# Rotary products on VectorE, row scaling and weight loads on ScalarE, and a reordered start, in an attention and retention block

## The chip, the cores and the metric

The kernel runs on one core of a Trainium2 chip. The metric is the device time of one execution in microseconds; for the kernel before, the median of three runs is 2031.37 us (2030.02, 2031.37 and 2033.79).

## What is computed

One encoder layer on 2048 tokens of width 1024, in fp32: a normalised input, one wide projection, a chunked attention branch, a retention branch whose queries and keys are rotated, and a gated merge.

```python
h = rms_norm(x, norm_gain)
q_a, k_a, v_a, g_a, q_r, k_r, v_r, g_r, m_a, m_r = split_columns(h @ w_in)
o_a = chunk_band_attention(q_a, k_a, v_a, rel_bias)
branch_a = (o_a * silu(g_a)) @ w_out_attn
qr, kr = rotary(q_r, positions), rotary(k_r, positions)
# rotary: concatenate [x1 * cos - x2 * sin, x1 * sin + x2 * cos]
o_r = retention_chunkwise(qr, kr, v_r, gn_gain)
branch_r = (o_r * silu(g_r)) @ w_out_ret
x = x + (sigmoid(m_a) * branch_a + sigmoid(m_r) * branch_r) @ w_out
return rms_norm(x, final_gain)
```

## The kernel before

**Split arithmetic.** Each fp32 operand of a large matmul is kept as a high half (a cast, `wh`) and a low half (the difference, `wl`), and three matmuls of halves replace one. `make` does this for a weight: the cast on ScalarE, the difference on VectorE or GpSimd `LO_LAG` = 4 steps later.

**Projection.** `w_in` is multiplied in chunks of 256 columns for 1024 tokens by Strassen's scheme: seven products of 12 matmuls a chunk (`PRODUCTS`). The activation parts stand ready in `R[0..6]`; the weight parts are two blocks of the raw weights or sums of them (`SUMS_OF`, t1 to t4, on GpSimd). Raw weights come by `load`, two loads a chunk of 512 KB into a ring of `RAWS` = 3 buffers, 9 and 8 products ahead (`RAW_LEADS`). The jobs are p0 and g0 for the first 1024 tokens, p1 and g1 for the second, and resident jobs for the output weights.

**Order of the work.** All engines' instructions are issued in program order through wrappers (`Ordered`, line 137 in the profile). One generator runs the products; `step()` issues three matmuls, a quarter of a product, and then whatever is due. `later(n, fn)` defers work by n steps, `put(lag, dst, src)` issues a store on SP that many steps later, `run_to(n)` runs steps up to n, and `prime(n)` prepares the weights of the first n products (in the running stretch three ahead, `AHEAD`).

**Start.** `start_up` takes the first 1024 tokens as xa and xb (512 each). Per block of 512 it squares the rows, forms the inverse root on VectorE (`chain`), scales the rows, transposes them on TensorE and writes the parts: `hi` and `lo` make R[0] to R[2], s1 to s3 the sums, and `to_parts` their halves. The second activation part's low half is called r11 below (`r_84` in the order's rows); s2 becomes s4 by subtracting the two halves of R[1] on GpSimd, eight operations.

**Second half.** During p0, `second_half` squares the other 1024 tokens and, in four pieces, fetches their rows (`xs`, 128x512), scales them on GpSimd, transposes them ten steps later (`pst`), combines and stores them; `reload` reads them back before p1.

**Rotation.** `ep_rotated` is run when both halves of a group of query or key columns are out of PSUM. For block b (512 tokens): two cross products with the sine table on GpSimd (t, 3 steps later), two own products with the cosine table (steps 7 and 8) and two sums (9 and 10) on VectorE. `keys` then transposes the rotated keys on TensorE in two halves (`trkr`, steps 15 and 19), and `parted` splits and stores them. The two blocks of a chunk pair follow each other, the odd one first. There are 16 rotations, eight of them of keys.

Of the kernel before, what the change touches and what calls it, by code (L numbers as in the profile page):

```python
# [21 lines left out]
P = 128  # L22
# [34 lines left out]
ATT_FILLS = (1.0, 1.0)  # L57
PV_LAG = 3
RET_FILLS = (2.1, 2.3)
RAW_LEADS = (9, 8)  # L60
TR_LATER = 16
YR_FROM = 14
# [5 lines left out]
def hybrid_kernel(  # L68
# [186 lines left out]
    class Chunk:  # L255
# [7 lines left out]
        def load(self, js=None):  # L263
            self.raw = self.raw or []
            for j in range(self.job.kh) if js is None else js:
                raw = wp.tile([P, 4, T], F32, tag="raw", bufs=RAWS, name=f"raw_{self.job.name}_{self.c}_{j}")
                dma(raw, self.job.stream(self.c, j))
                self.raw.append(raw)

        def half(self, j, c):  # L270
# [217 lines left out]
    def start_up():  # L488
# [88 lines left out]
        a11 = [E(f"a11_{k}") for k in range(4)]  # L577
        for k in range(4):
            act.activation(a11[k], ps[k], AF.Copy, scale=ng[:, k:k + 1])
        squares(xb, "b", 1, True)  # L580
        run_to(4)
        squares(xb, "b", 2, True)
        prime(3)
        ps = [TR(f"pa1_{k}") for k in range(4)]
        for k in range(4):
            turn(ps[k], k, xa, 1)
            hi(1, k, ps[k], 4 + k)
            lo(1, k, ps[k], 4 + k)
        for i in range(2):
            ch[1].b[f"b2{i + 1}"] = E(f"b2{i + 1}", shape=(P, 4, P))  # L590
        quarter(1, "b21")
# [4 lines left out]
        run_to(8)  # L596
        prime(4)
        a21 = [E(f"a21_{k}") for k in range(4)]
        squares(xb, "b", 3)
        run_to(12)  # L600
        tiny = ACC("tiny")
        nn["b"][1] = tiny[:, 0:4]
        chain("b", 0, 4)
        for f in (1, 0):
            for t in range(4):
                scale(xb, "b", t, f, t % 2)
        for dst in (0, 1, 3):
            ch[0].sum(*SUMS_OF[dst])
        run_to(16)
# [45 lines left out]
        for c in range(2):  # L655
            ch[c].sum(*SUMS_OF[2], E)
        run_to(28)
        for k in range(4):
            to_parts(5, k, s3[k])
        prime(9)  # L660
        for k in range(4):
            pool.tensor_tensor(s2[k], r32(R[1][0][:, k, :]), s2[k], ALU.subtract)
            pool.tensor_tensor(s2[k], r32(R[1][1][:, k, :]), s2[k], ALU.add)
        run_to(32)
        prime(10)
        for k in range(4):
            to_parts(3, k, s1[k])
        prime(11)
# [7 lines left out]
    def second_half(at):  # L676
# [25 lines left out]
        def piece(k):  # L702
            tiles = {}

            def fetch(i, f):
                a = tiles[i, f] = E(f"xs_{k}_{i}_{f}", shape=(P, 4, P))
                rows = x[0, (2 + i) * B:(3 + i) * B, 512 * f + k * P:512 * f + (k + 1) * P]
                dma(a, rows.rearrange("(t p) c -> p t c", p=P))
                later(8, lambda: scale(i, f))

            def scale(i, f):
                a = tiles[i, f]
                r = rs[:, 4 * i:4 * i + 4].unsqueeze(2).broadcast_to([P, 4, P])
                pool.tensor_tensor(a, a, r, ALU.mult)
                later(10, lambda: turn(i, f))

            def turn(i, f):
                a = tiles[i, f]
                ps = TR(f"pst_{k}_{i}_{f}")
                for t in range(4):  # L720
                    pe.transpose(ps[:, t * P:(t + 1) * P], a[:, t, :], ident)
                a = tiles[i, f] = a.rearrange("p t c -> p (t c)")
                later(1, lambda: act.activation(a, ps, AF.Copy, scale=ng[:, 4 * f + k:4 * f + k + 1]))

            def store(m, t, lag):
                put(lag, cscr[m][k], t)

            def first():
                s1 = tiles["s1"] = E(f"s1_{k}")
                pool.tensor_tensor(s1, tiles[1, 0], tiles[1, 1], ALU.add)  # L730
                store(2, tiles[1, 1], 2)
                store(3, s1, 4)

            def second():
                a11 = tiles[0, 0]
                s2 = tiles["s2"] = E(f"s2_{k}")
                dve.tensor_tensor(s2, tiles["s1"], a11, ALU.subtract)
# [12 lines left out]
            fetch(1, 0)  # L750
            later(3, lambda: fetch(1, 1))
            later(6, lambda: fetch(0, 0))
            later(10, lambda: fetch(0, 1))
            later(24, first)
            later(28, second)
            later(32, third)
# [42 lines left out]
    def ep_qa(cc, b, j, src, ps):  # L799
        p = 2 * cc + j  # L800

        def go():
            qh, ql = two(f"qa_{b}_{p}")
            act.mul(qh, src, -0.125)

            def rest():
                dve.scalar_tensor_tensor(ql, src, -0.125, r32(qh), ALU.mult, ALU.subtract)
                put(3, r32(qascr[p][b][:, :, 0, :]), halves(qh))
                put(3, r32(qascr[p][b][:, :, 1, :]), halves(ql))

            soon(2, rest)

# [2 lines left out]
    def ep_ka(cc, b, j, src, ps):  # L815
        p = 2 * cc + j

        def go():
# [3 lines left out]
            def rest():  # L822
                dve.tensor_tensor(kl, src, r32(kh), ALU.subtract)
                for i in range(2):
                    put(3, r32(kascr[2 * p + i][b][0:64, :]), r32(kh[64 * i:64 * i + 64, :]))
                    put(3, r32(kascr[2 * p + i][b][64:128, :]), r32(kl[64 * i:64 * i + 64, :]))

            soon(2, rest)

# [10 lines left out]
    def ep_va(cc, b, j, src, ps):  # L840
# [3 lines left out]
        def rest():  # L844
# [6 lines left out]

            def low(i):
                dve.tensor_tensor(vt[i][:, :, HD:P], pv[:, i], r32(vt[i][:, :, 0:HD]), ALU.subtract)
                put(3, r32(vascr[2 * p + i][b]), r32(vt[i]).rearrange("p t c -> p (t c)"))

            for i in range(2):
                later(1 + i, lambda i=i: high(i))
# [15 lines left out]
    def ep_rotated(kind):  # L873

        def epilogue(cc, b, j, src, ps):
# [7 lines left out]
            nm = f"{kind}_{cc}_{b}"  # L883
            ts = [E(f"t{n}_{nm}") for n in range(2)]

            def cross():
                for n in range(2):
                    pool.tensor_tensor(ts[n], xs[1 - n], s, ALU.mult)

            def own(n):  # L890
                dve.tensor_tensor(xs[n], xs[n], c, ALU.mult)
# [1 line left out]
            def both(n):  # L893
                dve.tensor_tensor(xs[n], xs[n], ts[n], ALU.add if n else ALU.subtract)

            later(3, cross)
            for n in range(2):
                later(7 + n, lambda n=n: own(n))
                later(9 + n, lambda n=n: both(n))
            (keys if kind == "k" else queries)(cc, b, xs, nm)  # L900

        return epilogue

    def parted(xs, nm, at, eng, dst):
# [7 lines left out]
        def low(n):  # L912
            eng.tensor_tensor(ws[n][1], xs[n], r32(ws[n][0]), ALU.subtract)
            for i in range(2):
                put(4, dst(i, n), halves(ws[n][i]))

        for n in range(2):
            later(at + n, lambda n=n: high(n))
            later(at + 4 + 2 * n, lambda n=n: low(n))

    def queries(cc, b, xs, nm):
        parted(xs, nm, 13, dve, lambda i, h: r32(qrscr[cc][b][:, :, :, h, i]).rearrange("u i c t -> (i c) u t"))

    def keys(cc, b, xs, nm):
        parted(xs, nm, 13, pool, lambda i, h: r32(krscr[cc][b][:, i, :, :, h]).rearrange("u i c t -> (i c) u t"))

        def turn(u):
            pk = TR(f"trkr_{nm}_{u}")
# [11 lines left out]
            def low(n):  # L940
                dve.tensor_tensor(
                    kt[n][:, :, :, HD:P], pk[:, 2 * n:2 * n + 2], r32(kt[n][:, :, :, 0:HD]), ALU.subtract
                )
                put(4, r32(kdscr[2 * cc + n][b][:, u]), r32(kt[n]).rearrange("p i t c -> p i (t c)"))

            for n in range(2):
                later(2 + n, lambda n=n: high(n))
                later(5 + n, lambda n=n: low(n))

        for u in range(2):  # L950
            later(15 + 4 * u, lambda u=u: turn(u))

    def ep_vr(cc, b, j, src, ps):
        h = 2 * cc + j
# [3 lines left out]
        def rest():  # L958
# [16 lines left out]
            def low():  # L975
                pool.tensor_tensor(vv[1], vc, r32(vv[0]), ALU.subtract)
                for n in range(2):
                    put(3, r32(vrscr[h][b][:, :, n, :]), r32(vv[n]))

            later(2, centred)  # L980
            later(4, high)
# [761 lines left out]
```

## Time and profile before

| | us |
|---|---|
| median of three runs | 2031.37 |
| profiled execution | 2029.79 |
| its span | 2028.0 |
| TensorE busy | 1937.3 |
| VectorE busy | 1363.4 |
| ScalarE busy | 881.5 |
| GpSimd busy | 943.1 |

The span runs from the first to the last instruction of one profiled execution; busy times are of that span. Most operations are recorded under the line of the wrapper that issues them, so rows are told apart by tile names: `wh_p` and `wl_p` are halves of weights of the p jobs, `t_p` the sums, `raw_p` the raw weights, `ps_p_x` and its kin the products' accumulators, `r` the activation parts, `u_p`, `c_p` and `xk` columns on their way out, `cs_k` the tables, `t_k` the cross products, `trkr_k` the transposed keys. The names in front of an arrow are outputs, those behind it inputs.

### The profile page before, as it was taken

What the parts mean: (1) busy time and instruction counts of PE and PEld (TensorE: products, weight loads), DVE (VectorE), ACT (ScalarE), POOL (GpSimd) and SP (SyncE); (2) the same over time, 40 slices, a digit from 0 to 9 for tenths busy, and PEclk for the clock granted to TensorE, in tenths of its full rate; (3) what the DMA queues carried; (4) which work ended last, traced back from release to release, by engine and by line L of the source; (5) the groups of instructions that cost most, each with busy time, mean ns of one, the idle gap of its engine ahead of it and who ended that gap; (6) DMA issues with size and microseconds to landing.
All of it is one profiled execution on the core that took longest, in us unless ns stands there. A gap on an engine that the chain in (4) does not pass through costs nothing.

```text
span 2028.0 us, 30428 instructions
## 1 busy us (share of the span) xinstructions
PE 1937.3 (96%) x9712; PEld 1611.1 (79%) x9712; DVE 1363.4 (67%) x2571; ACT 881.5 (43%) x1759; POOL 943.1 (47%) x765
## 2 busy tenths in 40 slices
PE   5899999999999999999999999999999999999998
PEld 4677777888888887777787888887888777888886
DVE  7968677677766667878777767765556644643554
ACT  5444343465555555333333555554455311322221
POOL 2644855555555676556664454454665134021000
PEclk9899999999999999999999999999999999999999
DMA  5376686755638887676784645554998899976664
GB/s 166 97 253 192 209 277 222 203 156 161 181 120 278 277 280 251 213 242 220 230 291 154 200 144 156 168 156 121 285 280 267 299 374 366 358 243 207 197 197 135
DMA packets 340912, 447.45 MB, mean 221 GB/s; under 512 B 30776, under 2 KB 194256, under 8 KB 340752
## 3 DMA queue, kind: packets, MB, share of 16 engines
q1 hardware_dynamic: 339712, 445.50, 68.9%
q8 instruction: 78, 1.28, 0.3%
q14 instruction: 82, 0.67, 0.1%
q10 hardware_dynamic: 1040, 0.00, 0.0%
HBM read 294.50 MB, written 150.89 MB: 220 GB/s over the span
## 4 chain that ended last, share of the span: by engine, by line
PE 77%; DVE 10%; DMA 5%; issue 4%; POOL 2%; ACT 1%; SPq 1%; DVEq 0%; POOLq 0%; ACTq 0%
PE ps_g_z L137 7%; PE ps_g_x L137 6%; PE ps_p_x L137 5%; PE ps_p_z L137 5%; PE po L137 4%; PE wide L137 3%; PE ps_g_w L137 3%; PE ps_g_v L137 3%; PE ps_g_y L137 3%; PE ps_p_w L137 3%; PE ps_p_v L137 3%; PE o L137 3%; PE tp L137 2%; PE ps_p_y L137 2%; DVE wl_p L137 2%
## 5 line engine op out<-in xcount | busy, mean ns | idle before, releaser
L137 POOL TENSOR_SCALAR pr<-pr,rsum 128x640 f32<-128x640 f32 (+4 forms) x128 | 96.5, 754 | 235.6 <-DVE rsum L137 98.6
L137 PE MATMUL ps_p_x<-r,wh_p 128*128 128x512 f32 x448 | 144.9, 404 | 4.3 <-DVE r L137 4.3
L137 PE MATMUL ps_p_z<-r,wh_p 128*128 128x512 f32 x448 | 141.7, 396 | 2.7 <-ACT wh_p L137 1.4
L137 PE MATMUL ps_g_z<-r,wh_g 128*128 128x512 f32 x448 | 142.4, 399 | 1.7 <-DVE c_g L137 1.3
L137 DVE CUSTOM_DVE_ANT_0 pr<-wide,bt 128x640 f32<-128x640 f32 (+4 forms) x128 | 94.3, 737 | 72.9 <-PE wide L137 65.2
L137 PE MATMUL ps_g_x<-r,wh_g 128*128 128x512 f32 x448 | 142.6, 399 | 0.0
L137 POOL TENSOR_TENSOR t_p<-raw_p,t_p 128x512 f32<-128x512 f32 x52 | 75.8, 1458 | 132.1 <-DVE wl_p L137 91.4
L137 ACT ACTIVATE pr<-pr,mn 128x640 f32<-128x640 f32 (+4 forms) x128 | 98.0, 766 | 80.5 <-DVE mn L137 80.5
L137 DVE TENSOR_TENSOR ptl<-tp,pth 128x384 fp32r<-128x384 f32 x168 | 95.7, 571 | 37.4 <-ACT pth L137 36.6
L137 ACT CAST pth<-tp 128x384 fp32r<-128x384 f32 x168 | 85.3, 514 | 75.5 <-PE tp L137 67.1
L137 DVE TENSOR_TENSOR wl_p<-t_p,wh_p 128x512 fp32r<-128x512 f32 x112 | 114.1, 1018 | 0.5 <-ACT wh_p L137 0.4
L1090 POOL TENSOR_TENSOR gr<-gr,ta 128x512 f32<-128x512 f32 x32 | 45.8, 1431 | 141.2 <-DVE gr L1089 81.6
L137 POOL TENSOR_TENSOR sl<-sm,sh 128x512 fp32r<-128x512 f32 x64 | 88.1, 1377 | 38.9 <-ACT sh L137 29.7
L137 PEld LDWEIGHTS ps_p_x<-r,wh_p 128*128 128x128 f32 x448 | 84.9, 193 | 22.8 <-DVE r L137 5.6
L137 PEld LDWEIGHTS tp<-ident,pr 128*128 128x128 f32 x560 | 69.6, 140 | 36.5 <-DVE ptl L137 8.5
L137 PEld LDWEIGHTS ps_p_z<-r,wh_p 128*128 128x128 f32 x448 | 82.1, 188 | 20.1 <-ACT wh_p L137 1.9
L137 PE MATMUL tp<-ident,pr 128*128 128x128 f32 x560 | 90.0, 274 | 7.4 <-DVE g L137 2.9
L137 PE MATMUL ps_p_x<-r,wl_p 128*128 128x512 f32 x224 | 89.7, 400 | 6.9 <-DVE wl_p L137 6.9
L137 PE MATMUL wide<-ka,qa 128*128 128x512 f32 (+2 forms) x448 | 94.0, 326 | 0.7 <-DVE mn L137 0.7
L137 DVE TENSOR_TENSOR sm<-sr,dm 128x512 f32<-128x512 f32 x64 | 44.2, 690 | 73.6 <-PE sr L137 43.9
L137 PE MATMUL po<-pth,va 128*128 128x256 f32 x336 | 92.7, 298 | 0.0
L137 ACT CAST wh_p<-t_p 128x512 fp32r<-128x512 f32 x112 | 69.1, 619 | 48.2 <-PE ps_p_z L137 24.0
(1183 smaller groups left out, 5930.2 us busy)
## 6 DMA issues: line engine op xcount, KB each, us to landing
raw_g<-in_w_in_dram SPq DMA_DIRECT2D x56, 512.0 KB, 5.2
raw_p<-in_w_in_dram SPq DMA_DIRECT2D x52, 512.0 KB, 5.0
qa<-qas SPq DMA_DIRECT2D x128, 128.0 KB, 2.9
qr<-qrs SPq DMA_DIRECT2D x128, 128.0 KB, 4.3
vr<-vrs SPq DMA_DIRECT2D x64, 256.0 KB, 4.4
ka<-kas SPq DMA_DIRECT2D x40, 256.0 KB, 3.4
va<-vas SPq DMA_DIRECT2D x40, 256.0 KB, 3.4
kds<-kdt_k SPq DMA_DIRECT2D x32, 256.0 KB, 5.0
```

The source lines that it names most:

```text
L137: return tc.keep_in_program_order(op(*a, **k))
L1090: pool.tensor_tensor(g, g, ta, ALU.add)
```

## The change

1. Rotary: the two cross products move to VectorE, one step apart. With `late` = 0 for odd blocks and 4 for even ones, a rotation's six operations stand at steps late + 1 to late + 6, the splitting at late + 8 (it was 13), the transposes at late + 11 and late + 14 (they were 15 and 19).
2. Rows of the second half are scaled on ScalarE, 128 columns at a time, and transposed six steps later instead of ten.
3. The raw weights of the Strassen jobs are loaded from ScalarE's queue, 108 loads; those of the resident jobs stay on SP.
4. Stores of queries, keys, values and parts are issued six steps after they are formed (three or four before), those of the second half's pieces four steps later.
5. In `start_up`, squares of two tiles of xb move behind r11, the inverse root and the row scales ahead of a run of steps, the preparation of products 9 and 10 ahead of and between the halves of part 5, and the second column block's values are kept (`a12`, four copies on ScalarE) so that s4 takes four GpSimd operations.

```diff
+ROT_LATE = 4
+PUT = 6
...
-                dma(raw, self.job.stream(self.c, j))
+                (dma if self.job.resident else act.dma_start)(raw, self.job.stream(self.c, j))
...
-        squares(xb, "b", 1, True)
         run_to(4)
-        squares(xb, "b", 2, True)
         prime(3)
...
             hi(1, k, ps[k], 4 + k)
             lo(1, k, ps[k], 4 + k)
+        a12 = [E(f"a12_{k}") for k in range(4)]
...
         a21 = [E(f"a21_{k}") for k in range(4)]
+        squares(xb, "b", 1, True)
         squares(xb, "b", 3)
-        run_to(12)
+        squares(xb, "b", 2, True)
         tiny = ACC("tiny")
         nn["b"][1] = tiny[:, 0:4]
         chain("b", 0, 4)
+        for k in range(4):
+            act.activation(a12[k], ps[k], AF.Copy, scale=ng[:, 4 + k:5 + k])
         for f in (1, 0):
             for t in range(4):
                 scale(xb, "b", t, f, t % 2)
+        run_to(12)
...
         run_to(28)
+        prime(9)
         for k in range(4):
             to_parts(5, k, s3[k])
-        prime(9)
+            if k == 1:
+                prime(10)
         for k in range(4):
-            pool.tensor_tensor(s2[k], r32(R[1][0][:, k, :]), s2[k], ALU.subtract)
-            pool.tensor_tensor(s2[k], r32(R[1][1][:, k, :]), s2[k], ALU.add)
+            pool.tensor_tensor(s2[k], a12[k], s2[k], ALU.subtract)
         run_to(32)
-        prime(10)
...
-                r = rs[:, 4 * i:4 * i + 4].unsqueeze(2).broadcast_to([P, 4, P])
-                pool.tensor_tensor(a, a, r, ALU.mult)
-                later(10, lambda: turn(i, f))
+                for t in range(4):
+                    later(t // 2, lambda t=t: act.mul(a[:, t], a[:, t], rs[:, 4 * i + t:4 * i + t + 1]))
+                later(6, lambda: turn(i, f))
...
-                put(lag, cscr[m][k], t)
+                put(lag + 4, cscr[m][k], t)
...
-                put(3, r32(qascr[p][b][:, :, 0, :]), halves(qh))
+                put(PUT, r32(qascr[p][b][:, :, 0, :]), halves(qh))
...
-            def cross():
-                for n in range(2):
-                    pool.tensor_tensor(ts[n], xs[1 - n], s, ALU.mult)
+            def cross(n):
+                dve.tensor_tensor(ts[n], xs[1 - n], s, ALU.mult)
...
-            later(3, cross)
+
+            late = 0 if b % 2 else ROT_LATE
             for n in range(2):
-                later(7 + n, lambda n=n: own(n))
-                later(9 + n, lambda n=n: both(n))
-            (keys if kind == "k" else queries)(cc, b, xs, nm)
+                later(late + 1 + n, lambda n=n: cross(n))
+                later(late + 3 + n, lambda n=n: own(n))
+                later(late + 5 + n, lambda n=n: both(n))
+            (keys if kind == "k" else queries)(cc, b, xs, nm, late)
...
-        parted(xs, nm, 13, pool, lambda i, h: r32(krscr[cc][b][:, i, :, :, h]).rearrange("u i c t -> (i c) u t"))
+    def keys(cc, b, xs, nm, late):
+        parted(xs, nm, late + 8, pool, lambda i, h: r32(krscr[cc][b][:, i, :, :, h]).rearrange("u i c t -> (i c) u t"))
...
-            later(15 + 4 * u, lambda u=u: turn(u))
+            later(late + 11 + 3 * u, lambda u=u: turn(u))
```

How the instructions stand is shown at three places. The first is VectorE at the first rotation of keys (`u_p_2_1229` and `c_p_2_1231` are the odd block's halves; `u_p_2_1152` and `xk_0_0_1250` the even block's; the wrapper's line is 137 before and 139 after). Before:

```order
L137 TENSOR_TENSOR u_p_2_1229<-ps_p_2_w,u_p_2_1229 128x512
L137 TENSOR_TENSOR wl_p_3_4_1257<-t_p_3_1190,wh_p_3_4_1256 128x512
L137 TENSOR_TENSOR u_p_2_1152<-ps_p_2_z,u_p_2_1152 128x512
L137 TENSOR_TENSOR wl_p_3_1_1287<-t_p_3_1192,wh_p_3_1_1286 128x512
L137 TENSOR_TENSOR u_p_2_1229<-u_p_2_1229,cs_k_1_0_1182 128x512
L137 TENSOR_TENSOR c_p_2_1231<-c_p_2_1231,cs_k_1_0_1182 128x512
L137 TENSOR_TENSOR u_p_2_1229<-u_p_2_1229,t_k_1_1277 128x512
L137 TENSOR_TENSOR wl_p_3_2_1310<-t_p_3_1214,wh_p_3_2_1309 128x512
L137 TENSOR_TENSOR c_p_2_1231<-c_p_2_1231,t_k_1_1278 128x512
L137 TENSOR_TENSOR xk_0_0_1250<-xk_0_0_1250,cs_k_0_0_1279 128x512
```

After:

```order
L139 TENSOR_TENSOR wl_p_3_4_1261<-t_p_3_1194,wh_p_3_4_1260 128x512
L139 TENSOR_TENSOR t_k_1_1281<-c_p_2_1235,cs_k_1_1_1183 128x512
L139 TENSOR_TENSOR t_k_1_1282<-u_p_2_1233,cs_k_1_1_1183 128x512
L139 TENSOR_TENSOR u_p_2_1233<-u_p_2_1233,cs_k_1_0_1182 128x512
L139 TENSOR_TENSOR c_p_2_1235<-c_p_2_1235,cs_k_1_0_1182 128x512
L139 TENSOR_TENSOR u_p_2_1154<-ps_p_2_z,u_p_2_1154 128x512
L139 TENSOR_TENSOR u_p_2_1233<-u_p_2_1233,t_k_1_1281 128x512
L139 TENSOR_TENSOR wl_p_3_1_1292<-t_p_3_1196,wh_p_3_1_1291 128x512
L139 TENSOR_TENSOR c_p_2_1235<-c_p_2_1235,t_k_1_1282 128x512
L139 TENSOR_TENSOR t_k_0_1312<-u_p_2_1154,cs_k_0_1_1284 128x512
L139 TENSOR_TENSOR wl_p_3_2_1317<-t_p_3_1218,wh_p_3_2_1316 128x512
L139 TENSOR_TENSOR t_k_0_1313<-xk_0_0_1254,cs_k_0_1_1284 128x512
```

The odd block's rotation is complete one weight's low half earlier, and its cross products stand on the same engine ahead of the own ones.

The second place is GpSimd there, after the change (`t_p` are sums of weights, `l_k` low halves of rotated keys):

```order
L139 TENSOR_TENSOR t_p_3_1294<-raw_p_3_1_1097,t_p_3_1196 128x512
L139 TENSOR_TENSOR l_k_1_0_1332<-u_p_2_1233,h_k_1_0_1331 128x512
L139 TENSOR_TENSOR t_p_4_1381<-raw_p_4_0_1258 128x512
L139 TENSOR_TENSOR t_p_4_1383<-raw_p_4_1_1289,t_p_4_1381 128x512
L139 TENSOR_TENSOR l_k_1_1_1340<-c_p_2_1235,h_k_1_1_1339 128x512
```

Before, four `t_k` products stood behind the first of these rows, and the first `l_k` operation behind both sums `t_p_4`.

The third is ScalarE at the same place, where the loads of the next chunk's raw weights now stand among the casts:

```order
L139 ACTIVATE xn_1_1173,ss_1011<-xn_1_1173 128x512
L139 DMA raw_p_4_0_1258<-in_w_in_dram 128x4x256
L139 CAST wh_p_3_4_1260<-t_p_3_1194 128x512
L139 DMA raw_p_4_1_1289<-in_w_in_dram 128x4x256
L139 CAST wh_p_3_1_1291<-t_p_3_1196 128x512
L139 CAST wh_p_3_2_1316<-t_p_3_1218 128x512
```

Before, both loads stood on SP between stores, tables and rows, and the casts followed one another.

## Rows read from the trace of the kernel before

**Rows 1.** The page's first lines: span, busy time by engine, the chain that ended last

```profile
span 2028.0 us, 30428 instructions
...
PE 1937.3 (96%) x9712; PEld 1611.1 (79%) x9712; DVE 1363.4 (67%) x2571; ACT 881.5 (43%) x1759; POOL 943.1 (47%) x765
...
PE 77%; DVE 10%; DMA 5%; issue 4%; POOL 2%; ACT 1%; SPq 1%; DVEq 0%; POOLq 0%; ACTq 0%
```

**Rows 2.** Windows of TensorE: start:end, length us, busy (instructions), granted clock, DMA share, GB/s

```profile
0.00:75.00 75.00, 46.85 (x177) 0.89 0.38 112
...
75.00:350.00 275.00, 258.75 (x1192) 0.98 0.71 224
...
800.00:1100.00 300.00, 281.85 (x1258) 0.98 0.72 234
```

**Rows 3.** Tile t_k (rotary products): count, ns min/median/max, starts; last, who waited (us, times)

```profile
L137 POOL TENSOR_TENSOR t_k<-u_p,cs_k x8: 1277/1733/1757, 108.0 to 1000.4; 128x512 f32<-128x512 f32 x8
...
L137 DVE TENSOR_TENSOR u_p<-u_p,t_k x8: 676/1212/1772, 112.1 to 1011.3; 128x512 f32<-128x512 f32 x8
...
  PE trkr_k L137: 14.4, 9
```

**Rows 4.** TensorE's waits: tile, releaser, us in total, times, longest us

```profile
PE ps_p_v L137 <- DVE wl_p L137: 7.1, 5, 4.1
...
PE ps_p_x L137 <- DVE wl_p L137: 6.9, 5, 2.6
...
PE ps_p_x L137 <- DVE r L137: 4.3, 1, 4.3
...
PE pst L137 <- POOL xs L137: 3.5, 2, 3.1
```

**Rows 5.** TensorE's timeline, 28 to 71: start, us, operation, [idle before it <- releaser]

```profile
30.73 0.80 PE L137 MATMUL ps_p_x<-r,wh_p 128*128 128x512 f32 x1 [4.26 <-DVE r L137]
...
31.75 1.05 PE L137 MATMUL ps_p_x<-r,wh_p 128*128 128x512 f32 x2
...
34.09 0.62 PE L137 MATMUL ps_p_x<-r,wh_p 128*128 128x512 f32 x2
...
36.84 0.61 PE L137 MATMUL ps_p_x<-r,wh_p 128*128 128x512 f32 x2
...
39.21 4.90 PE L137 MATMUL p<-ident,xb 128*128 128x128 f32 x24 [1.52 <-DVE xb L137]
...
68.75 0.79 PE L137 MATMUL ps_p_v<-r,wl_p 128*128 128x512 f32 x1 [4.05 <-DVE wl_p L137]
```

**Rows 6.** VectorE's timeline, from the start and from the first rotation of keys

```profile
26.60 1.75 DVE L137 CUSTOM_DVE_ANT_0 junk<-xb 128x512 bf16<-128x512 f32 x1
...
35.61 0.69 DVE L137 SCALAR_TENSOR_TENSOR l_qa<-ps_p_x,h_qa 128x512 fp32r<-128x512 f32 x1 [2.37 <-ACT h_qa L137]
...
62.96 4.06 DVE L137 TENSOR_TENSOR r<-s,r 128x512 fp32r<-128x512 f32 x4
...
110.43 1.79 DVE L137 TENSOR_TENSOR c_p<-c_p,cs_k 128x512 f32<-128x512 f32 x1
```

**Rows 7.** GpSimd's timeline, the same stretches

```profile
57.59 6.01 POOL L137 TENSOR_TENSOR a<-r,a 128x512 f32<-128x512 f32 x4 [0.63 <-DVE r L137]
...
108.05 3.62 POOL L137 TENSOR_TENSOR t_k<-u_p,cs_k 128x512 f32<-128x512 f32 x2
```

**Rows 8.** Tile xs (rows of the second half): the scaling

```profile
L137 POOL TENSOR_TENSOR xs<-xs,rs x16: 1032/1040/1488, 205.9 to 323.4; 128x512 f32<-128x512 f32 x16
```

**Rows 9.** ScalarE's timeline, two sizes of cast

```profile
102.87 0.61 ACT L137 CAST wh_p<-t_p 128x512 fp32r<-128x512 f32 x1
...
120.72 0.36 ACT L137 CAST kdt_k<-trkr_k 128x256 fp32r<-128x256 f32 x1
```

**Rows 10.** Tile raw_p (raw weights): the issues of its loads

```profile
L137 SPq DMA_DIRECT2D raw_p<-in_w_in_dram x52: 367/384/1547, 44.2 to 1058.6; - x52
```

**Rows 11.** SP's queue, its waits: releaser, us in total, times, longest us

```profile
SPq L137 <- DVE wl_p L137: 44.7, 28, 12.3
```

More of the change, by code (lines that the diff above doesn't have):

```diff
@@ L807, in rest @@
                 dve.scalar_tensor_tensor(ql, src, -0.125, r32(qh), ALU.mult, ALU.subtract)
-                put(3, r32(qascr[p][b][:, :, 0, :]), halves(qh))
-                put(3, r32(qascr[p][b][:, :, 1, :]), halves(ql))
+                put(PUT, r32(qascr[p][b][:, :, 0, :]), halves(qh))
+                put(PUT, r32(qascr[p][b][:, :, 1, :]), halves(ql))
             soon(2, rest)
@@ L824, in rest @@
                 for i in range(2):
-                    put(3, r32(kascr[2 * p + i][b][0:64, :]), r32(kh[64 * i:64 * i + 64, :]))
-                    put(3, r32(kascr[2 * p + i][b][64:128, :]), r32(kl[64 * i:64 * i + 64, :]))
+                    put(PUT, r32(kascr[2 * p + i][b][0:64, :]), r32(kh[64 * i:64 * i + 64, :]))
+                    put(PUT, r32(kascr[2 * p + i][b][64:128, :]), r32(kl[64 * i:64 * i + 64, :]))
             soon(2, rest)
@@ L853, in low @@
                 dve.tensor_tensor(vt[i][:, :, HD:P], pv[:, i], r32(vt[i][:, :, 0:HD]), ALU.subtract)
-                put(3, r32(vascr[2 * p + i][b]), r32(vt[i]).rearrange("p t c -> p (t c)"))
+                put(PUT, r32(vascr[2 * p + i][b]), r32(vt[i]).rearrange("p t c -> p (t c)"))
             for i in range(2):
@@ L914, in low @@
             for i in range(2):
-                put(4, dst(i, n), halves(ws[n][i]))
+                put(PUT, dst(i, n), halves(ws[n][i]))
         for n in range(2):
@@ L919, in parted, with queries @@
             later(at + 4 + 2 * n, lambda n=n: low(n))
-    def queries(cc, b, xs, nm):
-        parted(xs, nm, 13, dve, lambda i, h: r32(qrscr[cc][b][:, :, :, h, i]).rearrange("u i c t -> (i c) u t"))
-    def keys(cc, b, xs, nm):
-        parted(xs, nm, 13, pool, lambda i, h: r32(krscr[cc][b][:, i, :, :, h]).rearrange("u i c t -> (i c) u t"))
+    def queries(cc, b, xs, nm, late):
+        parted(xs, nm, late + 8, dve, lambda i, h: r32(qrscr[cc][b][:, :, :, h, i]).rearrange("u i c t -> (i c) u t"))
+    def keys(cc, b, xs, nm, late):
+        parted(xs, nm, late + 8, pool, lambda i, h: r32(krscr[cc][b][:, i, :, :, h]).rearrange("u i c t -> (i c) u t"))
         def turn(u):
@@ L943, in low @@
                 )
-                put(4, r32(kdscr[2 * cc + n][b][:, u]), r32(kt[n]).rearrange("p i t c -> p i (t c)"))
+                put(PUT, r32(kdscr[2 * cc + n][b][:, u]), r32(kt[n]).rearrange("p i t c -> p i (t c)"))
             for n in range(2):
@@ L977, in low @@
                 for n in range(2):
-                    put(3, r32(vrscr[h][b][:, :, n, :]), r32(vv[n]))
+                    put(PUT, r32(vrscr[h][b][:, :, n, :]), r32(vv[n]))
             later(2, centred)
```

## The prediction

> **What bounds the kernel now.** I read the page first: TensorE is busy 1937.3 of 2028.0 us, VectorE 1363.4, ScalarE 881.5, GpSimd 943.1, and the chain that ended last runs 77% over TensorE and 10% over VectorE [rows 1]. So no engine but TensorE is full, and a change of the other engines' work can win only what TensorE idles, about 91 us, and what it loses at its lower clock. The windows tell where that lies [rows 2]: the first 75 us (46.85 busy, clock 0.89), the first 1024 tokens' projection from 75 to 350 us (258.75 of 275, clock 0.98), and the second 1024 tokens' from 800 to 1100 us (281.85 of 300, clock 0.98). Idle there is 28.2, 16.3 and 18.2 us. The change edits these stretches and little else. Everything after them hangs on TensorE too, so what is won there should stay won.
>
> Then the waits, by what ended them. The tile view of the rotary products shows TensorE waiting 14.4 us in 9 places at the transposes of the rotated keys, the largest single item in the two projections [rows 3]. The list of TensorE's waits adds 7.1 and 6.9 us for low halves of weights, 3.5 us for scaled rows of x, and in the start 4.3 us for the low half of the second activation part [rows 4].
>
> **The start.** Removed from in front of r11 on VectorE are four squares of xb, each about 1.75 us (the last of them in [rows 6]), 6.8 us in a row; they now stand behind it. TensorE's 4.26 us wait at 30.73 ended by r11 [rows 5], so it goes. The squares are then in front of the norm of xb instead, but so they were before, and the norm also stood behind a low half that waited 2.37 us for ScalarE and began at 35.61 [rows 6]; it now stands ahead of it. With VectorE free 6.8 us earlier, the squares, the norm and the row scales end some 3 to 4 us earlier, and the transposes of xb, which began at 39.21 [rows 5], follow. I take 3.6 us, between 1.4 and the 4.26 of the wait. Four new ScalarE copies (a12) cost 4 x 0.6 us there, beside the norm on VectorE; if that cover is gone, they delay half of the row scales by at most 2.4 us, which is the lower end.
>
> Later in the start, the low half of a weight lands 4.05 us late at 68.75 [rows 5], behind four low halves of an activation part that took VectorE 4.06 us [rows 6]. Moving the preparation of products 9 and 10 among these takes two to four of the four away from in front: 3 us, with 0 and 4 as ends. Forming s2 in four GpSimd operations instead of eight saves one of two stretches of about 6 us [rows 7]; a wait follows only partly from it, and I take 0.9 (0 to 2). Together the start gives 7.5 us, between 4 and 12.
>
> **The rotations.** Removed are 32 GpSimd products, of 1.28 to 1.76 us [rows 3], and 32 come to VectorE. On VectorE an operation with both inputs in SBUF takes 0.68 us at its fastest and 1.77 us at its slowest in the same eight instructions [rows 3]: it is slow where a GpSimd product runs beside it, as the one at 110.43, 1.79 us, beside two that run from 108.05 to 111.67 [rows 6, 7]. That is 1.1 us per overlap. Before, a pair of key rotations is 8 VectorE operations, about half of them slow: 4 x 1.77 + 4 x 0.68 = 9.8 us, and each pair also waits for GpSimd's products to end. Now it is 12 operations: 8.2 us if all are fast. So VectorE does more instructions in less time. Odd blocks have their six operations at steps 1 to 6 and the transposes at 11; a step is three matmuls, a quarter of a product of 2.75 us (from 34.09 to 36.84 [rows 5]), so they have some 2.7 us of slack. Even blocks have steps 5 to 10 and 15. But the order puts sums of the next weights and the low half of the odd block's keys on GpSimd in that stretch; three such overlaps cost 3.3 us, and the even blocks should still be 1 to 3 us late. Of the 14.4 us I leave 4.5: 10 us won, between 0 and 14.4.
>
> On this the Trainium skill, "SBUF — State Buffer", section "Who interferes with whom", states that a VectorE instruction with two SBUF inputs contends with a GpSimd instruction that reads SBUF, by an exclusive lock whose order of issue decides who blocks. The trace agrees (0.68 against 1.77 us), but the rule also speaks against putting the whole rotation on VectorE, since each moved product is of the kind that is locked out; by it alone the sum would lose its 10 us, and the time would be some 2013 us.
>
> Low halves of weights outside the start wait 9.9 us (7.1 + 6.9 - 4.05 [rows 4, 5]); they queue on VectorE behind the same slow operations. Half goes: 5 us (0 to 9.9). After a stall TensorE runs at half its clock for a while: two matmuls took 1.05 us right after the 4.26 us wait and 0.62 us later [rows 5], which are the levels 1.2 and 2.4 GHz. At a mean clock of 0.98 the two projections lose 2% of 575 us, 11.5 us [rows 2]. With over half of the stalls gone I take 6 us back (2 to 9).
>
> **The rows of x on ScalarE.** Sixteen GpSimd products of 1.04 us [rows 8] become 64 on ScalarE of a quarter the size. No row has that size: 128x256 took 0.36 and 128x512 0.61 us [rows 9], so a straight line gives 0.24, and the bounds are 0.15 (a quarter of 0.61) and 0.36: 15 us in all (10 to 23). ScalarE is busy 43% and TensorE does not wait for it there. The transposes waited 3.5 us for GpSimd's scaling [rows 4]; I take 2 of it (0 to 3.5). If the rows land late, ScalarE stands still with its casts, which is part of the rival below.
>
> **Weight loads on ScalarE's queue.** The 52 loads for the first kind of job took 0.38 us of issue each on SP [rows 10], and I take the same for the 56 of the gates: 108 leave SP, 41 us more on ScalarE, spread over 1400 us, ahead of casts that are prepared three products, 8 us, before their use. That cover hides an issue. SP waited 44.7 us at 28 loads for a buffer that VectorE still read [rows 11]; what stood behind these loads on SP (tables, rows, stores) is freed, but no wait of TensorE in the projections was for such a load, so I win nothing. On ScalarE a load stands later than it did on SP, mostly behind the release of its buffer. A few will wait; I charge 2.5 us, one wait of the size of the 1.52 us at 39.21 [rows 5] and a smaller one; the bounds are 0 and the rival. **Stores six steps behind** move only where SP issues them; nothing reads them for tens of us. Tiles are held two to three steps, 2 us, longer, which I cost at nothing, since no new tile wait follows from the order; without that cover it is one 2 us wait per rotation.
>
> **The sum.** 7.5 + 10 + 5 + 6 + 2 - 2.5 = 28 us. The profiled execution took 2029.8 us, 1.6 below the median of 2031.4; against the median, 2003.4, and I say 2003.
>
> **Rivals.** *VectorE becomes the bound of the rotations* (0.17). Everything that was won there hangs on twelve operations fitting between two products; if GpSimd's sums meet nearly all of them, a pair takes 12 x 1.77 = 21 us, as long as two chunks' slack cannot cover. Against it: GpSimd has 48 operations fewer, so fewer to meet. Then the start's 7.5 us and some clock stay, the transposes keep most of their 14.4 us, and the time is 2015 to 2027.
>
> *ScalarE held by its loads: slower* (0.10). A load in ScalarE's order that waits for a buffer, or for an earlier transfer, holds each cast behind it, and a row of x that lands late does the same in the second half's pieces. SP's 44.7 us at 28 loads is what such waiting amounts to where it is free [rows 11]; the same on ScalarE eats the 8 us of cover in some chunks. Each late cast stops TensorE and halves its clock. The point from which it decides is 32 us of stall over 108 loads, 0.3 us per load; at 0.5 us per load it is 54 us and 2003 + 54 = 2057 us. Against it: in the order most loads stand behind the operation that frees their buffer. Beside this the Trainium skill, "DMA: Bandwidth & Descriptors", section "Anatomy of one DMA — SWDGE (gpsimd) path", says that DMA engines do not wait on semaphores and that any such wait happens on the issuing sequencer; no run here yet shows it for ScalarE.
>
> *All stalls go* (0.10): transposes, low halves and clock wholly recovered, 12 + 14.4 + 9.9 + 9 + 3.5 = 49 us, 1982 us.
>
> *The gains pay the costs* (0.08): the transposes' wait moves to the low halves, whose operations now queue behind more of VectorE's, while the start alone improves and ScalarE costs as much: 2027 to 2035 us.
>
> **How the numbers follow.** My forecast (1990 to 2015) has 0.55. A measurement here tells 0.2%, 4 us, from no change. Faster is the forecast, the VectorE rival and the full recovery, 0.82; same 0.08; slower 0.10. The range of 8 in 10 runs from 1986, which leaves out half of the full recovery, to 2029, which leaves out the slower case and part of the even one.
>
> **What would show it.** Right: TensorE's first projection matmul after r11 without a wait near 30 us; xb's transposes near 35.6; key transposes waiting under 6 us in all, VectorE's rotary operations mostly at 0.68 us; no wait of casts for loads on ScalarE above 2 us; TensorE's idle in the three windows down from 63 to about 40 us and their clock up to 0.99. Wrong: rotary operations at 1.77 us and the transposes' 14.4 us kept or moved to the low halves; or ScalarE's waits ending in a raw load or in rows of x, with TensorE waiting for high halves, which it hardly does now.

## The result, and the profile after

The changed kernel took 2020.16 us in the median of four runs, against 2030.69 us for the kernel before beside it: a ratio of 0.9945, 95% interval 0.9927 to 0.9962. That is 11 us faster where 28 were forecast: the sign was right, the size was not, and the time is inside the stated range. One execution of an experiment below, the one with later transposes, took 5718 us and is left out of its ratio. The profiled execution has a span of 2016.9 us against 2028.0 [rows 1]. The page after:

```profile
span 2016.9 us, 30327 instructions
...
PE 1934.7 (96%) x9712; PEld 1607.6 (80%) x9712; DVE 1367.9 (68%) x2603; ACT 899.3 (45%) x1827; POOL 874.4 (43%) x713
```

VectorE did 32 operations more, as forecast, for 4.5 us more of busy time, where the rotation part had less time for more operations. To see where time was won, the same six matmuls are read in both timelines of TensorE: one at the end of a product of the start, the first of the third chunk of p0, the first of its last chunk, the retention's first scores, a wait of p1's first chunk, and one near p1's end. Before:

```profile
75.99 0.62 PE L137 MATMUL ps_p_v<-r,wh_p 128*128 128x512 f32 x2
...
87.58 0.62 PE L137 MATMUL ps_p_x<-r,wh_p 128*128 128x512 f32 x2
...
340.88 0.62 PE L137 MATMUL ps_p_x<-r,wh_p 128*128 128x512 f32 x2
...
619.50 0.71 PE L137 MATMUL sr<-qr,kr 128*128 128x256 f32 x4 [1.61 <-DMA qr<-qrs]
...
802.33 0.73 PE L137 MATMUL ps_p_z<-r,wh_p 128*128 128x512 f32 x2 [1.44 <-ACT wh_p L137]
...
1079.97 0.63 PE L137 MATMUL trva<-ident,c_p 128*128 128x128 f32 x4 [0.50 <-DVE c_p L137]
```

After, with one new wait at 70.40 between the first two:

```profile
64.04 0.62 PE L139 MATMUL ps_p_v<-r,wh_p 128*128 128x512 f32 x2
...
70.40 1.19 PE L139 MATMUL ps_p_z<-r,wh_p 128*128 128x512 f32 x2 [5.51 <-DVE u_p L139]
...
82.82 0.62 PE L139 MATMUL ps_p_x<-r,wh_p 128*128 128x512 f32 x2
...
325.64 0.62 PE L139 MATMUL ps_p_x<-r,wh_p 128*128 128x512 f32 x2
...
606.16 1.19 PE L139 MATMUL sr<-qr,kr 128*128 128x256 f32 x4 [3.60 <-DMA qr<-qrs]
...
792.25 0.73 PE L139 MATMUL ps_p_z<-r,wh_p 128*128 128x512 f32 x2 [1.42 <-ACT wh_p L139]
...
1068.92 0.63 PE L139 MATMUL trva<-ident,c_p 128*128 128x128 f32 x4 [0.50 <-DVE c_p L139]
```

The lead, time before minus time after, is 12.0 us ahead of the new wait, 4.8 behind it, 15.2 at the end of p0, 13.3 at the first scores, 10.1 at the start of p1, and 11.1 both near its end and at the end of the span. So 15 us were won by 341 us, 5 were given back up to p1, and p1, where half of the rotary gain was expected, gave 1.

**The transposes still wait.** The tile view of the rotary products after:

```profile
L139 DVE TENSOR_TENSOR t_k<-u_p,cs_k x8: 684/1780/1787, 101.2 to 991.3; 128x512 f32<-128x512 f32 x8
...
  PE trkr_k L139: 13.5, 12
```

The last row is what TensorE waited at the transposes: 14.4 us [rows 3] became 13.5, where 4.5 were forecast. At the first rotation VectorE's timeline after shows why:

```profile
106.59 1.77 DVE L139 TENSOR_TENSOR t_k<-u_p,cs_k 128x512 f32<-128x512 f32 x1
108.29 1.78 DVE L139 TENSOR_TENSOR wl_p<-t_p,wh_p 128x512 fp32r<-128x512 f32 x1
109.99 0.68 DVE L139 TENSOR_TENSOR t_k<-xk,cs_k 128x512 f32<-128x512 f32 x1
110.70 1.67 DVE L139 TENSOR_TENSOR xk<-xk,cs_k 128x512 f32<-128x512 f32 x1
112.30 1.77 DVE L139 TENSOR_TENSOR u_p<-u_p,cs_k 128x512 f32<-128x512 f32 x1
```

and beside it GpSimd's:

```profile
106.20 1.62 POOL L139 TENSOR_TENSOR l_k<-u_p,h_k 128x512 fp32r<-128x512 f32 x1 [3.81 <-DMA xn<-in_x_dram]
107.78 1.74 POOL L139 TENSOR_TENSOR t_p<-raw_p 128x512 f32<-128x512 f32 x1
110.20 1.62 POOL L139 TENSOR_TENSOR t_p<-raw_p,t_p 128x512 f32<-128x512 f32 x1 [0.68 <-POOL t_p L139]
111.79 1.73 POOL L139 TENSOR_TENSOR l_k<-c_p,h_k 128x512 fp32r<-128x512 f32 x1
```

Four GpSimd operations, two low halves of the odd block's keys and two weight sums, meet four operations of VectorE on the even block's way, three of its rotation and a weight's low half. The one at 109.99, which began before GpSimd's at 110.20, kept its 0.68 us.

**The start's new wait.** The 5.51 us at 70.40 ended with the drain of an accumulator (the operation that takes a finished product out of it), the last of these rows of VectorE, behind the two others:

```profile
61.73 6.25 DVE L139 TENSOR_TENSOR r<-a,r 128x512 fp32r<-128x512 f32 x4
67.90 1.75 DVE L139 TENSOR_TENSOR wl_p<-t_p,wh_p 128x512 fp32r<-128x512 f32 x1
69.57 0.68 DVE L139 TENSOR_TENSOR u_p<-ps_p_v,u_p 128x512 f32<-128x512 f32 x1
```

The first row is the four low halves of activation part 3. GpSimd formed part 6's at the same time:

```profile
59.30 8.14 POOL L139 TENSOR_TENSOR r<-a,r 128x512 fp32r<-128x512 f32 x4 [3.76 <-ACT r L139]
```

**The retention's start.** On SP's queue after, and on ScalarE's:

```profile
599.79 2.52 SPq L139 DMA_DIRECT2D qr<-qrs  x4
605.55 0.34 SPq L139 DMA_DIRECT2D kd<-kds  x1
```

```profile
599.26 0.41 ACTq L139 DMA_DIRECT2D raw_g<-in_w_in_dram  x1
602.73 0.37 ACTq L139 DMA_DIRECT2D raw_g<-in_w_in_dram  x1
```

Two 512 KB loads of the gates' weights now start among the queries' transfers. Before, they stood on SP behind all of the first operands. The scores start 3.9 us after the last query's issue (1.9 before). SP's next issue comes 3.2 us after the queries', and waited for one of these loads to land. Over the whole span SP waited for landings of the gates' weights, before and after:

```profile
SPq L137 <- DMA raw_g<-in_w_in_dram: 4.3, 7, 1.3
```

```profile
SPq L139 <- DMA raw_g<-in_w_in_dram: 56.3, 20, 4.8
```

TensorE's granted clock was lower there as well. Its window from 600 to 800 us, before and after:

```profile
600.00:800.00 200.00, 196.02 (x1110) 1.00 0.81 256
```

```profile
600.00:800.00 200.00, 191.24 (x1055) 0.98 0.88 269
```

### The profile page after: what moved, and what is told of

Read it like the earlier page. It is cut to its first block, busy times and chain, and to the rows that moved or that the text cites. A ratio compares the mean times of both kernels' runs of the same rounds, so it can differ in the third digit from the quotient of the medians.

```text
span 2016.9 us, 30327 instructions
## 1 busy us (share of the span) xinstructions
PE 1934.7 (96%) x9712; PEld 1607.6 (80%) x9712; DVE 1367.9 (68%) x2603; ACT 899.3 (45%) x1827; POOL 874.4 (43%) x713
## 4 chain that ended last, share of the span: by engine, by line
PE 75%; DVE 10%; DMA 8%; issue 3%; ACT 2%; SPq 1%; POOL 0%; DVEq 0%; ACTq 0%; POOLq 0%
PE ps_g_z L139 7%; PE ps_g_x L139 6%; PE ps_p_x L139 5%; PE ps_p_z L139 5%; PE po L139 4%; PE wide L139 3%; PE ps_g_v L139 3%; PE ps_g_w L139 3%; PE ps_g_y L139 3%; PE ps_p_w L139 3%; PE tp L139 3%; PE o L139 2%; PE ps_p_v L139 2%; PE ps_p_y L139 2%; DVE wl_p L139 2%
## 5 line engine op out<-in xcount | busy, mean ns | idle before, releaser
L139 DVE TENSOR_TENSOR wl_p<-t_p,wh_p 128x512 fp32r<-128x512 f32 x112 | 104.5, 933 | 2.6 <-ACT wh_p L139 2.6
L139 POOL TENSOR_TENSOR wl_g<-t_g,wh_g 128x512 fp32r<-128x512 f32 x56 | 76.8, 1372 | 38.4 <-ACT wh_g L139 33.1
```

Source lines behind the costliest of these rows:

```text
L139: return tc.keep_in_program_order(op(*a, **k))
```

## The experiments

Sixteen kernels in four groups; ratios are to the kernel before, with 95% intervals.

**One part of the change alone**, each on the kernel before. The rotary part:

```diff
...
-            later(3, cross)
...
+                later(late + 1 + n, lambda n=n: cross(n))
...
```

> The kernel before with the rotary part of the change alone: cross products on VectorE, the new steps for rotations, splits and transposes. As forecast (the rotation fits): the transposes of rotated keys wait under 6 us in all and the time falls by 12 to 18 us. Theory now (the even block's six operations meet the odd block's low halves and the next weights' sums on GpSimd, so the stall only changes its place): the transposes still wait 11 to 15 us, and the time falls by 0 to 5 us.

Ratio 0.994 (0.9917 to 0.9962), the whole change's gain. The transposes waited 14.7 us, about as long as before and in the change, but the time fell by more than that theory gave: low halves of weights outside the start waited 4.1 us instead of 9.9, and the clock from 262 to 345 us rose from 0.96 to 1.00. Each theory was half right.

The rows of x:

```diff
...
-                pool.tensor_tensor(a, a, r, ALU.mult)
...
+                    later(t // 2, lambda t=t: act.mul(a[:, t], a[:, t], rs[:, 4 * i + t:4 * i + t + 1]))
...
```

> The kernel before with only the scaling of the second half's rows moved to ScalarE. As forecast: 2 us of the transposes' 3.5 us go, and the time falls by 1 to 4 us. Theory now (sixteen GpSimd operations of the first projection also slowed VectorE's low halves of weights, and each stall there was followed by half-clock matmuls): the waits at 282 and 330 us both go, and the time falls by 5 to 9 us.

Ratio 1.001 (0.9995 to 1.0026): both missed. In its tile view of the rows, the first two of these lines are ScalarE's price and what ScalarE stood still for, the third who waited:

```profile
L137 ACT ACTIVATE xs<-xs,rs x64: 387/393/407, 210.6 to 331.6; 128x128 f32<-128x128 f32 x64
...
  DMA xs<-in_x_dram: 14.5, 6
...
  PE pst L137: 6.5, 2
```

SP brought the rows behind stores and raw weights, ScalarE waited for them in order, and TensorE's 3.5 us for scaled rows became 6.5. Its profiled execution also has the wait in the start that is told of with the stores below.

The weight loads:

```diff
-                dma(raw, self.job.stream(self.c, j))
+                (dma if self.job.resident else act.dma_start)(raw, self.job.stream(self.c, j))
```

> The kernel before with only the raw weights' loads of the Strassen jobs on ScalarE's queue. As forecast: 0 to 3 us slower. Theory now (a load issued early from the second queue lands between the retention's first operands, and SP's issues wait for loads that take 5 us to land): the wait of the first retention scores for queries grows from 1.6 to 3 us or more, SP waits over 60 us for landings of raw weights where it waited under 10 us, and the time is 0 to 4 us slower. Rival (loads were late on SP): 2 to 5 us faster.

Ratio 1.002 (1.0005 to 1.0036): slower by about 4 us, over the forecast's 0 to 3 and at the end of the theory's 0 to 4. The scores' wait for queries was 7.2 us in 4 places over both halves (3.3 in 2 before, 6.6 in 5 in the change), SP waited 60.0 us in 24 places for landings of the gates' weights, and TensorE's window from 600 to 800 us lost 4.4 us of its 196.02:

```profile
600.00:800.00 200.00, 191.63 (x1075) 0.98 0.82 248
```

The reordered start (the hunks of `start_up` alone):

```diff
-        squares(xb, "b", 1, True)
         run_to(4)
-        squares(xb, "b", 2, True)
...
```

> The kernel before with only the reordered start. As forecast: 4 to 12 us faster, likeliest 7.5. Theory now (the start wins 11 us up to the products of part 3 and gives some 5 us back there, because the low halves of parts 3 and 6 are now formed at the same time on VectorE and GpSimd and slow each other, and an accumulator's drain stands behind them on VectorE): a wait of 4 to 6 us for a drain near 70 us, and 4 to 6 us faster at the end.

Ratio 0.9986 (0.9969 to 1.0004), the 5.5 us wait at 70 us in place as expected. The time, some 3 us under the kernel before and not told from it, missed both ranges.

The later stores:

```diff
...
-                put(3, r32(qascr[p][b][:, :, 0, :]), halves(qh))
+                put(PUT, r32(qascr[p][b][:, :, 0, :]), halves(qh))
...
```

> The kernel before with only the later stores (six steps, and four more for the second half's pieces). As forecast, and by every theory of now: within 0.2% of the kernel before, since TensorE waits for no store in the projections. Rival (tiles held 2 us longer hold back the casts that write them): 2 to 6 us slower.

Ratio 1.0026 (1.001 to 1.0043), the rival by the number. But its profiled execution loses 5 of its 8 us before 88 us, by a 5.5 us wait for a drain at the same place as above. The kernel with the rows alone, whose start is instruction for instruction the one of before, had that wait as well (5.54 us), while the kernel before did not in its profiled execution. The same four low halves, in the kernel before and in the one with the rows alone:

```profile
70.30 3.56 DVE L137 TENSOR_TENSOR r<-a,r 128x512 fp32r<-128x512 f32 x4
```

```profile
69.29 6.84 DVE L137 TENSOR_TENSOR r<-a,r 128x512 fp32r<-128x512 f32 x4
```

So this wait comes and goes with how two engines happen to meet, and the parts alone can carry 5 us of it: with the start of before, two of seven profiled kernels have it; with the reordered start and part 6 on GpSimd, all six.

**One part of the change undone or repaired.** All loads back on SP:

```diff
-                (dma if self.job.resident else act.dma_start)(raw, self.job.stream(self.c, j))
+                dma(raw, self.job.stream(self.c, j))
```

> The changed kernel with the raw weights' loads back on SP. If the loads on ScalarE's queue delay the retention's first operands and SP's issues: the wait of the first scores falls from 3.6 to 1.6 us or less and the time falls by 1 to 4 us against the changed kernel (2016 to 2019 us). If the loads were the part that paid: 2 to 6 us slower than the changed kernel (2022 to 2026).

Ratio 0.9941 (0.9921 to 0.9961): no difference to the change, so both expectations missed. The scores' wait fell (2.3 us in 2), and from the end of p0 to the start of p1 0.6 us of lead were lost, where the change lost 5.1. What was saved there was lost in p0, where scaled rows were waited for 7.1 us instead of 1.5. The loads pay for the rows' part and cost about as much in the retention.

Loads of the p jobs alone on ScalarE's queue:

```diff
-                (dma if self.job.resident else act.dma_start)(raw, self.job.stream(self.c, j))
+                (act.dma_start if self.job.name[0] == "p" else dma)(raw, self.job.stream(self.c, j))
```

> The changed kernel with ScalarE's queue loading raw weights for the two p jobs alone; those of the gates, which run beside attention and retention, go back to SP. If the loads pay in the first projection (SP is free for the rows of x) and cost in the retention (the next weights land between its first operands): the lead of 15 us after the first projection stays, the 5 us lost between 606 and 798 us shrink to 1 to 2, and the time falls by 3 to 5 us (2015 to 2017). Rival (the retention's start waits for transfers that begin when the attention ends, so what is won before is lost there): within 2 us of 2020.

Ratio 0.992 (0.9898 to 0.9941). The scores' wait went back to 3.2 us in 2, and TensorE was busy 193.97 us from 600 to 800 where the change had 191.24. Its interval overlaps the change's: the mechanism is seen in the trace, a gain in the times is not shown.

Transposes of keys later:

```diff
-            later(late + 11 + 3 * u, lambda u=u: turn(u))
+            later(15 + 4 * u if b % 2 else 18 + 4 * u, lambda u=u: turn(u))
```

> The changed kernel with the transposes of rotated keys later: steps 15 and 19 for odd blocks (11 and 14 in the change) and 18 and 22 for even ones (15 and 18). If the stall is only the transposes coming before VectorE has finished: their wait falls from 13.4 us to under 4 us, and the time falls by 8 to 13 us against the changed kernel (2007 to 2012). Rival (VectorE is the bound there and the stall moves to low halves of weights or to drains of accumulators): the transposes' wait falls, the other waits grow by as much, and the time stays within 3 us of 2020.

Ratio 0.9878 (0.9854 to 0.9903), 12 to 14 us under the change. In its list of TensorE's waits (us, times, longest) the transposes are down to one:

```profile
PE ps_p_x L139 <- DVE wl_p L139: 7.5, 8, 1.7
...
PE trkr_k L139 <- DVE u_p L139: 1.1, 1, 1.1
```

The window of p1 went from 286.75 us busy at 0.98 in the change to

```profile
800.00:1100.00 300.00, 289.38 (x1321) 1.00 0.73 230
```

The rival holds for a part: low halves of weights, the first row, waited 7.5 us, against 2.9 in the change.

Low halves of the odd block's keys later:

```diff
...
-            later(at + 4 + 2 * n, lambda n=n: low(n))
+            later(at + 4 + more + 2 * n, lambda n=n: low(n))
...
```

`more` is 8 for the keys of odd blocks and 0 for the others.

> The changed kernel with the low halves of the odd block's rotated keys (on GpSimd) formed eight steps later, behind the even block's rotation. If GpSimd's operations slow the even block's rotation by 1.1 us for each overlap: two of four overlaps go, the even blocks' operations at 1.7 us fall from about four a pair to two, their transposes wait 2 us less a pair, and the time falls by 4 to 9 us (2011 to 2016). If VectorE's own number of operations is the cause: no change in the waits (13 us) and within 2 us of 2020.

Ratio 0.9902 (0.9874 to 0.9931). The tile view of the rotary products, with only GpSimd's two operations a pair moved out of the way:

```profile
L139 DVE TENSOR_TENSOR xk<-xk,t_k x4: 678/678/1758, 112.7 to 993.0; 128x512 f32<-128x512 f32 x4
...
  PE trkr_k L139: 5.4, 9
```

13.5 us became 5.4, with as many operations on VectorE as in the change: the overlap is the cause, not the count.

Part 6 off GpSimd, in place:

```diff
-            to_parts(6, k, s2[k], pool)
+            to_parts(6, k, s2[k])
```

> The changed kernel with the low halves of part 6 on VectorE behind those of part 3, not on GpSimd beside them. If their overlap causes the 5.5 us wait at 70 us: part 3's four low halves take 2.5 us in place of 6.3, the wait falls to under 2 us, and the time falls by 3 to 6 us (2014 to 2017). Rival (VectorE is full there and the drain comes as late behind more operations): the wait stays over 4 us and the time within 2 us of 2020.

Ratio 0.9934 (0.9912 to 0.9956): not to be told from the change. Its VectorE shows part 3 at 0.6 us an operation as expected, and part 6 slow in its turn, beside a low half and sums of weights on GpSimd:

```profile
61.29 2.48 DVE L139 TENSOR_TENSOR r<-a,r 128x512 fp32r<-128x512 f32 x4
...
65.98 6.78 DVE L139 TENSOR_TENSOR r<-a,r 128x512 fp32r<-128x512 f32 x4
72.69 0.68 DVE L139 TENSOR_TENSOR u_p<-ps_p_v,u_p 128x512 f32<-128x512 f32 x1
```

The wait moved to the next drain (5.39 us at 73.51). So part 6 was also put behind both drains:

```diff
-        for k in range(4):
-            to_parts(6, k, s2[k], pool)
-        run_to(40)
+        run_to(42)
+        for k in range(4):
+            to_parts(6, k, s2[k])
```

> The changed kernel with part 6 formed six steps later and wholly on VectorE, behind both drains of the accumulators of part 5's products. The run that only took part 6 off GpSimd made part 3 fast (2.5 us) and had the 5.4 us wait one product later, for the second drain, which stood behind part 6. If these drains behind slow low halves are the whole of it: no wait over 2 us between 60 and 80 us, and the lead at the second chunk is 8 to 11 us where the changed kernel has 4.8; the time falls by 3 to 6 us (2014 to 2017). Rival (part 6 itself is late then, or the lead is lost at the rows of x and at the retention's start, whose transfers do not come earlier): less than 2 us at the end.

Ratio 0.9915 (0.9893 to 0.9936). The largest wait left there is 2.78 us at 73.91, over the 2 us expected, and the lead at the third chunk is 8.1 us in place of 4.8; the interval just overlaps the change's.

**Together.** The three repairs, later transposes, part 6 behind the drains and the gates' loads on SP, are the edits above:

> The changed kernel with three repairs together: transposes of rotated keys later (steps 15 and 19, 18 and 22), part 6 later and on VectorE, and the gates' raw weights on SP. If the three costs are separate they add: 12 us of the transposes, 3 to 6 of the start and 3 to 5 of the retention, 1998 to 2003. If the first projection's gains are partly lost where the rows of x or the retention's operands land, 2003 to 2008.

2003.1 us (2001.87 to 2004.71), ratio 0.9857 (0.9837 to 0.9878): faster than both kernels, at the edge between the two expectations. Its windows of the start and of p1:

```profile
0.00:75.00 75.00, 50.15 (x209) 0.95 0.37 112
...
800.00:1100.00 300.00, 291.04 (x1330) 1.00 0.75 234
```

From it, the stores early again (three steps everywhere, where some had four before, and the pieces' four steps taken back), and the rows on GpSimd as before:

```diff
-PUT = 6
+PUT = 3
...
```

> The kernel with the three repairs (2003), with stores as before: three steps late, and the second half's pieces not four steps later. If later stores cost in themselves (0.26% alone, with a 5.5 us wait at the start's accumulators in the profiled run, which the kernel before also has in some runs): 3 to 6 us faster than 2003. If that was the chance state of the start's waits: within 3 us of 2003.

```diff
...
-                    later(t // 2, lambda t=t: act.mul(a[:, t], a[:, t], rs[:, 4 * i + t:4 * i + t + 1]))
...
+                pool.tensor_tensor(a, a, r, ALU.mult)
...
```

> The kernel with the three repairs, with the rows scaled on GpSimd and transposed ten steps later, as before. If the rows on ScalarE pay once SP is free of raw weights: 3 to 7 us slower than 2003, with the waits for scaled rows or low halves of weights near 270 to 330 us back. If they do not pay: within 2 us of 2003.

Ratios 0.9868 (0.9844 to 0.9892) and 0.9861 (0.9837 to 0.9885): neither is told from 0.9857. In the time neither stores nor rows are seen to pay or cost here, to within some 5 us. In the trace the stores do something: scaled rows were waited for 6.0 us in 2 places with early stores, 2.2 with late ones.

**Pairs on the kernel before.** Rows and loads:

> The kernel before with rows scaled on ScalarE and all 108 raw loads on its queue. Alone the rows' part was 0.1% slower, with ScalarE idle 14.5 us for rows that stood on SP behind stores and raw weights, and TensorE 6.5 us for scaled rows. If the two parts need each other: the transposes' wait falls to under 2 us, the lead grows by 4 to 8 us between 200 and 341 us, some 6 us are lost in the first retention as with the loads alone, and the time is within 4 us of 2030, 3 to 7 us under the sum of both alone (2036). If they are independent: 2034 to 2038 and a wait for scaled rows of 4 us or more.

Ratio 1.001 (0.9997 to 1.0024). Scaled rows were still waited for 6.0 us in 2 places: the theory that the loads alone free SP for the rows falls. Inside the change it was 1.5 us, and with the stores put back in the repaired kernel 6.0, which speaks for the later stores: on SP the rows stand behind stores and loads alike. It isn't settled, as the kernel with the odd blocks' low halves later waited 5.8 us for rows, with stores late and loads on ScalarE. Rotary with the later transposes:

> The kernel before with the rotary on VectorE and the transposes of keys at steps 15 and 19, 18 and 22, and no other part. If the step chosen for the transposes is what held the rotary part back: their wait falls from 13 us to under 3, and the time is 8 to 13 us under the rotary part's 2020 (2008 to 2012). If the late transposes need the other parts (free GpSimd, SP): 2014 to 2020.

Ratio 0.9889 (0.9861 to 0.9918), transposes not waiting: this one part, with the right step, is worth twice the whole change.

## Why the prediction was wrong

- **The rotations** (10 us) failed at "three such overlaps cost 3.3 us, and the even blocks should still be 1 to 3 us late. Of the 14.4 I leave 4.5". 13.5 us were left. The overlaps were seen, and so was the lateness: of the 13.5 us, 11.1 are even blocks', 2.8 a pair, with three or four of the six operations slow in each. But there are four pairs, and 1 to 3 us a pair is 4 to 12: I took the lower end of it for the whole. "VectorE does more instructions in less time" failed too: the 12 operations of a pair of key rotations took 13.2 us and not 8.2 (19 of the 48 were slow), where 8 had taken 10.8. The step at which the transposes stand decided: later by three to five steps, the 12 us appeared (0.9878), and with GpSimd's two operations moved, the wait lost 8 of its 13.5 us. The change moved GpSimd's low halves of the odd block's keys five steps forward, into the even block's rotation; I saw them in the order and priced them too low. The rival "VectorE becomes the bound of the rotations" (2015 to 2027) came by its time and by the transposes that keep their wait, but not by its condition: far from nearly all twelve operations were slow, and the wait fell without taking any of them off VectorE.
- **On the rule of the Trainium skill**, "SBUF — State Buffer", section "Who interferes with whom": it was set against the change, and the trace after agrees for the most part. In the windows of p0 and p1, all 58 of VectorE's 128x512 operations with both inputs in SBUF that took over 1.5 us began while a GpSimd operation was running. But 14 that began so, and 42 that GpSimd joined only after their start, stayed near 0.7 us: what an overlap cost depended mostly on which of the two began first. The 2013 us worked out by it was nearer than my sum, and yet 7 us off, since other terms failed as well.
- **The start** (7.5 us) gave 4.8. The waits named there did go, and TensorE was 12 us ahead by 64 us: xb's transposes began at 33.40, 5.8 us earlier where 3.6 were forecast. The step that failed is the one left out, what is late next. Parts 3 and 6 came to be formed side by side, and 7 us went to the drain behind them: 5.5 of waiting, the rest at the lower clock after it (1.19 us for two matmuls at 70.40, 0.62 at 64.04). The range given, 4 to 12, is also not the sum of its terms' ends, which is 1.4 to 10.3.
- **Low halves of weights** (5 us): 9.9 us became 2.9, so 7. **Clock** (6 us): the windows of p0 and p1 went from 0.98 and 0.98 to 0.99 and 0.98, some 2.75 us by these rounded figures; the window from 600 to 800 us, which the forecast left out, fell from 1.00 to 0.98, some 4 us.
- **Rows on ScalarE**: the price, 0.15 to 0.36 us, missed: an operation of 128x128 took 0.39 us, 25 us in all instead of 15. The 2 us of waits forecast as won were won (3.5 to 1.5).
- **Loads**: the charge (2.5 us) was looked for in ScalarE's casts; it came to 4 to 5 us in the retention, wait and clock together, which I had not read at all, having written that the change edits the projections "and little else". SP's 44.7 us at 28 waits [rows 11] was misread too: 19 of these waits, 41.1 us, stood before loads, nine before stores.
- The sum as measured: 4.8 in the start, 10.4 in the rest of p0, 5.2 lost up to p1, 1 won in p1, 11 us. The forecast's terms with what they measured, 4.8 + 0.9 + 7 + 2.75 + 2 - 5.2, give an estimate of 12.3. TensorE's idle time in the windows of [rows 2] went from 62.6 to 49.0 us, where 40 was the sign of being right.

## What to carry to other kernels

An operation moved off a shared engine leaves its old neighbours behind: list what the other engine now does in the same steps, count every overlap, and price each at the slow row. When a result comes earlier or later, the step at which its consumer stands in TensorE's order must be set anew; here that one number was worth as much as the change. And a load moved to a second queue is early somewhere: look at what it now lands among, in every phase that uses it.

## What was not expected of the hardware

A 128x128 scaling on ScalarE by a value per row took 0.39 us (64 of them), more than a 128x256 cast (0.36 us) [rows 9]. VectorE's four low halves of one part took 2.5, 3.6, 6.2 or 6.8 us, and the same code 3.6 or 6.8, by what GpSimd did beside them. Beside the second queue's loads the first queue's transfers took longer: the queries', issued next to two weight loads, held the scores for 3.6 us instead of 1.6, and for 1.6 again with these loads back on SP. This agrees with the Trainium skill, "DMA: Bandwidth & Descriptors", section "Issuing engines are not separate DMA queues", that DMAs of all issuing engines run interleaved on the same engines.
